# Taking the POOL engine out of the front of a two-block transformer kernel, and spreading its modulation sums

## The chip, the cores and the metric

One core of a Trainium2 chip runs the whole program as one launch. The metric is the device time of a launch in microseconds (us); the kernel before took 2275.55 us (median of 3 runs, 2274.65 to 2276.33).

## The reference

Two blocks follow each other on 256 latent tokens of width 1024. The change lies in the first part of the first block, called the front here: the modulation vectors, the input projection and the two token mixers.

```python
m_l = silu(c) @ w_ada + b_ada                      # 6 x 1024 numbers: shift, scale, gate, twice
u_l = modulate(x, sh1_l, sc1_l) @ w_in             # 256 x 4128; the same for 256 context tokens: u_c
u_c = modulate(ctx, sh1_c, sc1_c) @ w_in
mix_c, mix_l = token_mixer(u_c, u_l, ...)          # HGRN2 (4 heads of 128), GLA (4 heads, in column order)
x = layer_norm(ALPHA * x + g1_l * (mix_l @ w_out), ...)
y_l = peer(modulate(x, sh2_l, sc2_l), ...)         # 16384 experts; then the second block
```

Each mixer is a gated linear recurrence, scanned forwards and backwards over the context and then the latent tokens.

## The kernel before

**Products of three.** Every float32 product is made of three matmuls: weight and activation are each split into a high part, rounded to the matmul's format, and the rest (`hi`, `lo`). The class `Stream` (L251 on) brings all weights in tiles of 128x1024 (512 KB) through one ring of four buffers `raw` and one DMA queue, SP's. `split_to` makes `wh` on ScalarE (L296) and `wl = raw - wh` on VectorE or on POOL (L297), which of the two is the letter "s" or "p" of the tile in `PROJ_MODES`, one pair of letters for each of the 16 groups of 256 columns of `w_in`. A `raw` buffer is free for the next load when its `wl` is made.

**Modulation sums.** The first 2048 columns of `w_ada` are multiplied on TensorE (`ada1_gen`, L521). 24 of the other 32 tiles come through the same ring with mode "r": `ada2_step` (L610) multiplies a tile by the row `crow` on VectorE and sums it along its rows, and its `raw` buffer is free after that. `ADA_PLAN` says after which of the 16 groups how many of these tiles stand; a tile is summed when its group's products are evacuated.

**Projection.** `fm_gen` (L618) makes 256 columns of features, `tm_gen` (L659) 256 columns with tokens on the partitions. The forget gates come first (4 groups of 512 tokens, evacuated at L680 to L684), then the values of the first mixer. The rest (queries, the GLA columns, the output gates) is a chain of generators from which `together` takes one piece, or several, between the steps of the mixers, after the list `FILL`.

**Mixers.** `mixer_states` scans the context, and `mixer` goes through nine levels L = 128, 64, 1, 32, 16, 8, 4, 2, 0. `prep(L)` makes four differences of scanned decays on VectorE (L802 to L805), two exponentials on ScalarE (L806, L807), the product with the keys on VectorE (L811, L812 or L809) and the product of `Qt` with the queries, L820, on POOL. For L = 1 the keys are copied on POOL (L818, L819). `scores` multiplies `Kt` and `Qt` on TensorE (L832) and puts the result into `SB` (L838 on ScalarE, or L840 on VectorE). `decays_g` (L940 to L944) makes the decays of the second mixer in the middle of the first, and L888, L891 write the outputs. After that come the output projection `wout` (from L992), layer norms and the expert stage.

**Column order.** For the GLA part the latent half of the split activations `xh`, `xl` is copied in column order into `hh`, `hl` by 16 casts (L905) on POOL.

**Order of instructions.** The order on each engine is not the program's: a scheduler sets it before the run, and each engine then works in that order, waiting at an instruction until what it reads is there.

Three stages are used below. Stage 1 is 61.65 to 187.30 us (from the first evacuated gate to the first L940), stage 2 to 238.5 us (the first L802 of the second mixer), stage 3 to 299.7 us (the first L992).

Of the kernel before, what the change touches and what calls it, by code (L numbers as in the profile page):

```python
# [8 lines left out]
F32 = mybir.dt.float32  # L9
# [3 lines left out]
AF = mybir.ActivationFunctionType  # L13
OP = mybir.AluOpType
# [9 lines left out]
             "gq": (2560, 256), "gk": (2816, 256), "gv": (3072, 512), "gg": (3584, 512), "gl": (4096, 32)}  # L24
W_IN_ORDER = ("hff", "hfb", "hi", "hq", "gl", "gk", "gq", "gv", "hg", "gg")
N_ADA = 24
ADA_PLAN = (0, 3, 3, 3, 3, 3, 3, 3, 3, 0, 0, 0, 0, 0, 0, 0, 0)

VEC = {}
_n = 0  # L30
# [13 lines left out]
OHB = 4  # L44
MIX_ORDER = 'PPPSPPPSSSSSSSSSMMSSSMSSMMMMMMMMMAASAAAAAPPPAAAPPPPPPPFFFFFPPPPFFFPPPPPPRRVFF'
EARLY = (9, 9, 7)
PROJ_MODES = ['ss', 'ss', 'pp', 'ps', 'sp', 'ss', 'ps', 'ss', 'ss', 'sp', 'pp', 'pp', 'sp', 'pp', 'pp', 'pp']
FILL_N = (8, 9, 17, 37, 53)
MODES = ("sssp", "sssp")
FILL = (3, 4, 1, 4, 3, 4, 2, 6, 5, 3, 3, 0, 0, 1, 3, 1, 3, 2, 2, 1, 2, 1)  # L50
# [125 lines left out]
def build(tc, A, out):  # L176
    nc = tc.nc
    V, S, T, G = nc.vector, nc.scalar, nc.tensor, nc.gpsimd

    with ExitStack() as ctx:  # L180
# [17 lines left out]
        for name in W_IN_ORDER:  # L198
# [3 lines left out]
            for g in range(n // 256):  # L202
                for half in range(2):
                    specs.append((A["win"][gi * 2 + half], PROJ_MODES[gi][half]))
                if gi == 1:
                    specs[1], specs[2] = specs[2], specs[1]
                for _ in range(ADA_PLAN[gi]):
                    specs.append((A["wa2"][na], "r"))
# [140 lines left out]
        def bc(ap, shape):  # L349
            return ap.to_broadcast(shape)  # L350
# [109 lines left out]
        with ExitStack() as fctx:  # L460
# [145 lines left out]
            def ada2_step(c):  # L606
                w = W.get("r")
                j = nada[0]
                nada[0] += 1
                V.scalar_tensor_tensor(w, w, 1.0, c, op0=OP.mult, op1=OP.mult, accum_out=mada[:, 16 + j:17 + j])  # L610

            def ada2_some():
                for _ in range(ADA_PLAN[ngroup[0]]):
                    ada2_step(crow)
                ngroup[0] += 1
# [40 lines left out]
            def colmajor(ap):  # L656
                return ap.rearrange("p (r w) -> p w r", w=64)
# [109 lines left out]
            def mixer(tg, nh, q, ks, a, v, Sc, sc, m0, between={}):  # L767
# [7 lines left out]
                b = []  # L775
# [11 lines left out]
                def prep(L):  # L787
                    Kt = tl("Kt", [4, 256], "Kt", 2)[:, 0:nh]
                    if L:
                        n = 128 // L  # L790
                        Qt = tl("Qt", [4, 256], "Qt", 2)[:, 0:nh]
                        sh = [128, nh, n, L]
                        kf0, _ = halves(ks[0][:, 0], L)
                        _, kb1 = halves(ks[1][:, 0], L)
                        K0, K1 = halves(Kt, L)
                        Q0, Q1 = halves(Qt, L)
                        if L > 1:
                            bf0, bf1 = halves(b[0], L)
                            bb0, bb1 = halves(b[1], L)
                            rf = bc(bf0[:, :, :, L - 1:L], sh)  # L800
                            rb = bc(bb1[:, :, :, 0:1], sh)
                            V.tensor_tensor(K0, rf, bf0, OP.subtract)  # L802
                            V.tensor_tensor(K1, rb, bb1, OP.subtract)
                            V.tensor_tensor(Q1, bf1, rf, OP.subtract)
                            V.tensor_tensor(Q0, bb0, rb, OP.subtract)  # L805
                            S.activation(out=Qt, in_=Qt, func=AF.Exp, scale=sc)  # L806
                            S.activation(out=Kt, in_=Kt, func=AF.Exp, scale=sc)  # L807
                            if same:
                                V.tensor_tensor(Kt, Kt, ks[0][:, 0], OP.mult)  # L809
                            else:  # L810
                                V.tensor_tensor(K0, K0, kf0, OP.mult)  # L811
                                V.tensor_tensor(K1, K1, kb1, OP.mult)  # L812
                        else:
                            _, af1 = halves(a[0][:, 0], L)
                            ab0, _ = halves(a[1][:, 0], L)
                            S.activation(out=Q1, in_=af1, func=AF.Exp, scale=sc)
                            S.activation(out=Q0, in_=ab0, func=AF.Exp, scale=sc)
                            G.tensor_copy(K0, kf0)  # L818
                            G.tensor_copy(K1, kb1)  # L819
                        G.tensor_tensor(Qt, Qt, q, OP.mult)  # L820
                    else:
                        V.tensor_tensor(Kt, ks[0][:, 0], ks[1][:, 0], OP.add)
                        Qt = q
                    return L, Kt, Qt
# [77 lines left out]
            xph, xpl = hh, hl  # L902
            for a, b in ((xph, xh), (xpl, xl)):
                for k in range(8):
                    G.tensor_copy(a[:, k, :].rearrange("p (w r) -> p w r", r=4), colmajor(b[:, k, 0:256].bitcast(F32)))  # L905

            nc.sync.dma_start(wgk, A["wgk"])

# [39 lines left out]
            def gate_ev(gain):  # L948
                def ev(f, ps):
                    if not gate:  # L950
# [8 lines left out]
                              for g in range(2)], gl_gen(), fm_gen(512, ev, 0, 1),  # L959
                            fm_gen(256, lambda f, ps: S.activation(out=gq[:, f, :].rearrange("p (w r) -> p w r", r=4),  # L960
                                                                   in_=colmajor(ps[:, 0:256]), func=AF.Copy, scale=0.125), 0, 2),
# [35 lines left out]
            for k in st1.end(eps1[:, 0:1], [xlat[:, k] for k in range(8)]):  # L997
                n, o, g, b = xlat[:, k], x1[:, k], vc("lng")[:, k:k + 1], bcen[:, k:k + 1]
# [8 lines left out]
            m2, r = tl("m2", [256], "b0"), tl("r2m", [256], "b1")  # L1007
# [16 lines left out]
        with ExitStack() as ectx:  # L1024
# [155 lines left out]
            for i2 in range(128):  # L1180
                hi, lo = W.get("s")
                p = PM()[:, 0:256]
# [37 lines left out]
            p = PS()  # L1220
# [36 lines left out]
            for i2 in range(125):  # L1257
                w = W.get("s")
# [7 lines left out]
            w = [W.get("s") for _ in range(3)]  # L1266
# [524 lines left out]
```

## Time and profile before

| what | before |
|---|---|
| median of 3 runs | 2275.55 us |
| the profiled execution, its own time | 2275.68 us |
| its span, first to last instruction | 2272.9 us |
| PE (matmul) busy | 2174.4 us, 96% |
| VectorE (DVE) busy | 1562.2 us, 69% |
| ScalarE (ACT) busy | 1166.6 us, 51% |
| POOL busy | 490.7 us, 22% |
| mean granted clock of TensorE | 0.981 |

A busy PE is not a PE at its peak: matmuls overlap, and one that waits behind another counts as busy, so work is better read from counts of matmuls. PE is the matmul row of TensorE, PEld its weight loads. The granted clock is a share of full speed (1.00 is 2.4 GHz). "idle" in a group of instructions is the time its engine stood still just before them, with what ended it.

### The profile page before, as it was taken

To read this page: it belongs to the slowest core of one execution; us is meant where nothing else is said; L and a number is where in the kernel's file an instruction comes from. 1 tells how busy PE (TensorE), PEld (TensorE's weight loads), DVE (VectorE), ACT (ScalarE), POOL (GpSimd) and SP (SyncE) were. 2 spreads that over 40 slices of the span, in tenths; PEclk is the share of its full clock that TensorE was granted. 3 is DMA by queue.
4 is the path that set the end of the run, shared out by engine and by line. 5 is a ranking of instruction groups with operands and counts; after the bars stand their busy time and mean duration, and the time that the engine had idled before them with its cause. 6 is when DMAs were issued, how large, how long until landed. Compare 5 with 4: busy or idle time off the path is not lost.

```text
span 2272.9 us, 40224 instructions
## 1 busy us (share of the span) xinstructions
PE 2174.4 (96%) x15660; PEld 2039.1 (90%) x15660; DVE 1562.2 (69%) x2786; ACT 1166.6 (51%) x2016; POOL 490.7 (22%) x464
## 2 busy tenths in 40 slices
PE   6898889899999999999989999999999999899998
PEld 4788779899999998888879999899999999889998
DVE  6897879963778866666665556786557555778554
ACT  4545655344444455555545445675446444676443
POOL 2224422222988810000010002110001000402000
PEclk9999999999999999999999999999999999999999
DMA  6652124555444457666555554344564556234664
GB/s 266 213 186 75 56 84 142 162 177 183 148 142 147 145 182 238 213 194 195 194 183 168 175 175 140 97 149 149 177 179 153 173 170 198 94 120 130 186 180 127
DMA packets 101999, 367.37 MB, mean 162 GB/s; under 512 B 11440, under 2 KB 13360, under 8 KB 100528
## 3 DMA queue, kind: packets, MB, share of 16 engines
q1 hardware_dynamic: 101808, 364.81, 50.6%
q8 instruction: 122, 2.00, 0.4%
q14 instruction: 69, 0.57, 0.1%
HBM read 363.72 MB, written 1.05 MB: 160 GB/s over the span
## 4 chain that ended last, share of the span: by engine, by line
PE 78%; DVE 12%; issue 3%; ACT 3%; POOL 2%; DMA 2%; SPq 0%; DVEq 0%; POOLq 0%; ACTq 0%
PE main L336 18%; PE main L335 18%; PE main L334 18%; PE aux L1254 5%; PE aux L1256 5%; PE aux L1255 5%; DVE wl L297 3%; PE aux L1144 3%; DVE raw L610 1%; POOL wl L297 1%; ACT wh L296 1%; PE aux L832 1%; DVE X L1076 1%; DVE X L1074 1%; DMA raw<-wa 1%
## 5 line engine op out<-in xcount | busy, mean ns | idle before, releaser
L296 ACT ACTIVATE wh<-raw 128x1024 fp32r<-128x1024 f32 (+1 forms) x630 | 659.4, 1047 | 702.0 <-PE main L335 348.0
L297 DVE TENSOR_TENSOR wl<-raw,wh 128x1024 fp32r<-128x1024 f32 (+1 forms) x589 | 724.9, 1232 | 382.0 <-ACT wh L296 381.5
L336 PE MATMUL main<-hh,wl 128*128 128x256 f32 (+1 forms) x2808 | 806.7, 288 | 20.3 <-DVE wl L297 19.9
L334 PE MATMUL main<-hh,wh 128*128 128x256 f32 (+1 forms) x2808 | 810.5, 289 | 12.2 <-DVE hh L444 6.1
L335 PE MATMUL main<-hl,wh 128*128 128x256 f32 (+1 forms) x2808 | 805.4, 287 | 1.5 <-DVE hl L448 0.7
L336 PEld LDWEIGHTS main<-hh,wl 128*128 128x128 f32 x2808 | 534.7, 190 | 26.1 <-DVE wl L297 23.7
L334 PEld LDWEIGHTS main<-hh,wh 128*128 128x128 f32 x2808 | 533.8, 190 | 16.8 <-DVE hh L444 7.0
L335 PEld LDWEIGHTS main<-hl,wh 128*128 128x128 f32 x2808 | 532.9, 190 | 3.8 <-DVE hl L448 2.0
L396 POOL TENSOR_TENSOR acc<-acc,sqk 128x272 f32<-128x272 f32 (+1 forms) x29 | 37.2, 1284 | 1207.6 <-ACT sqk L389 1207.5
L1138 POOL TENSOR_SCALAR oh<-cst,slotT 128x128 f32<-128x128 f32 x256 | 209.1, 832 | 38.4 <-PE aux L1144 32.6
L334 PE MATMUL main<-ah,wh 128*128 128x272 f32 (+1 forms) x704 | 201.7, 286 | 0.0
L335 PE MATMUL main<-al,wh 128*128 128x272 f32 (+1 forms) x704 | 201.3, 286 | 0.0
L336 PE MATMUL main<-ah,wl 128*128 128x272 f32 (+1 forms) x704 | 200.6, 285 | 0.0
L1254 PE MATMUL aux<-wh,xsh 128*128 128x512 f32 x512 | 199.3, 390 | 0.0
L1255 PE MATMUL aux<-wl,xsh 128*128 128x512 f32 x512 | 199.3, 389 | 0.0
L1256 PE MATMUL aux<-wh,xsl 128*128 128x512 f32 x512 | 199.2, 389 | 0.0
L297 POOL TENSOR_TENSOR wl<-raw,wh 128x1024 fp32r<-128x1024 f32 x41 | 112.9, 2755 | 302.1 <-ACT wh L296 301.4
L339 ACT ACTIVATE xsh<-X 128x256 fp32r<-128x256 f32 x128 | 53.7, 420 | 165.8 <-PE aux L1255 163.9
L336 PEld LDWEIGHTS main<-ah,wl 128*128 128x128 f32 x704 | 132.4, 188 | 0.0
L334 PEld LDWEIGHTS main<-ah,wh 128*128 128x128 f32 x704 | 132.3, 188 | 0.0
L335 PEld LDWEIGHTS main<-al,wh 128*128 128x128 f32 x704 | 132.2, 188 | 0.0
L1255 PEld LDWEIGHTS aux<-wl,xsh 128*128 128x128 f32 x512 | 96.1, 188 | 20.3 <-DVE wl L297 0.3
(507 smaller groups left out, 3246.0 us busy)
## 6 DMA issues: line engine op xcount, KB each, us to landing
raw<-uT SPq DMA_DIRECT2D x128, 512.0 KB, 3.6
raw<-pv SPq DMA_DIRECT2D x128, 512.0 KB, 4.2
raw<-ffn_gate SPq DMA_DIRECT2D x88, 512.0 KB, 3.6
raw<-ffn_up SPq DMA_DIRECT2D x88, 512.0 KB, 3.7
raw<-win SPq DMA_DIRECT2D x72, 512.0 KB, 3.7
raw<-ffn_down SPq DMA_DIRECT2D x64, 512.0 KB, 3.6
raw<-wa SPq DMA_DIRECT2D x32, 512.0 KB, 4.5
raw<-wout SPq DMA_DIRECT2D x24, 512.0 KB, 3.6
```

The costliest lines, as they stand in the source:

```text
L296: S.activation(out=hi[:, :n], in_=t[:, :n], func=AF.Copy)
L297: (G if mode == "p" else V).tensor_tensor(lo[:, :n], t[:, :n], hi[:, :n].bitcast(F32), OP.subtract)
L334: T.matmul(o, lh, rh, start=start, stop=False)
L335: T.matmul(o, lh, rl, start=False, stop=False)
L336: T.matmul(o, ll, rh, start=False, stop=stop)
L339: S.activation(out=hi, in_=src, func=AF.Copy)
L396: (G if self.k < (5 if self.pe == 7 else 2) else V).tensor_tensor(self.acc2, self.acc2, q, OP.add)
L1138: G.tensor_scalar(oh1[:, j], iota, slotT[0][:, t0 + j:t0 + j + 1], None, op0=OP.is_equal)
L1144: T.matmul(pg[:, 128 * j:128 * j + 128], oh1[:, j], oh2[:, j], start=True, stop=True)
L1254: T.matmul(y, x[0][:, c], w[0][:, f], start=(i2 == 0), stop=False)
L1255: T.matmul(y, x[0][:, c], w[1][:, f], start=False, stop=False)
L1256: T.matmul(y, x[1][:, c], w[0][:, f], start=False, stop=(i2 == 127))
```

## The change

`PROJ_MODES` becomes "ss" for all 16 groups: the 17 `wl` of the projection that POOL made go to VectorE. L820 goes to VectorE, the two key copies of L = 1 and the 16 casts of L905 to ScalarE. `ADA_PLAN` had three sums after each of groups 1 to 8, and has one after groups 1 to 4 and two after groups 5 to 14, 24 as before. Up to the end of stage 3 POOL keeps only one multiplication of the input normalisation (L580).

```diff
-ADA_PLAN = (0, 3, 3, 3, 3, 3, 3, 3, 3, 0, 0, 0, 0, 0, 0, 0, 0)
+ADA_PLAN = (0, 1, 1, 1, 1, 2, 2, 2, 2, 2, 2, 2, 2, 2, 2, 0, 0)
...
-PROJ_MODES = ['ss', 'ss', 'pp', 'ps', 'sp', 'ss', 'ps', 'ss', 'ss', 'sp', 'pp', 'pp', 'sp', 'pp', 'pp', 'pp']
+PROJ_MODES = ['ss'] * 16
...
-                            G.tensor_copy(K0, kf0)
-                            G.tensor_copy(K1, kb1)
-                        G.tensor_tensor(Qt, Qt, q, OP.mult)
+                            S.activation(out=K0, in_=kf0, func=AF.Copy)
+                            S.activation(out=K1, in_=kb1, func=AF.Copy)
+                        V.tensor_tensor(Qt, Qt, q, OP.mult)
...
             for a, b in ((xph, xh), (xpl, xl)):
                 for k in range(8):
-                    G.tensor_copy(a[:, k, :].rearrange("p (w r) -> p w r", r=4), colmajor(b[:, k, 0:256].bitcast(F32)))
+                    S.activation(out=a[:, k, :].rearrange("p (w r) -> p w r", r=4), in_=colmajor(b[:, k, 0:256].bitcast(F32)), func=AF.Copy)
```

The order on the engines moves with it. The first piece is VectorE at the start of stage 1, where the first gates are evacuated (L682, L684 scale `gat` and `kx`); "-" is the order before, "+" the new one:

```order
-L610 SCALAR_TENSOR_TENSOR raw,mada<-raw,crow 128x1024 x3
+L297 TENSOR_TENSOR wl<-raw,wh 128x1024 x2
+L610 SCALAR_TENSOR_TENSOR raw,mada<-raw,crow 128x1024
 L682 TENSOR_SCALAR gat_113<-gat_113,lbt 128x2x256
 L684 TENSOR_SCALAR kx_115<-kx_115,lbt 128x2x256
 L682 TENSOR_SCALAR gat_113<-gat_113,lbt 128x2x256
```

Three sums stood ahead of the second group's gates; now two splits and one sum do. By the first L940, VectorE's order has 19 splits and 14 sums where it had 11 and 24, and six L820.

The second place is VectorE at level L = 16 of the first mixer, late in stage 1. Before:

```order
L802 TENSOR_TENSOR Kt<-bl_1164 128x32x16
L803 TENSOR_TENSOR Kt<-bl_1169 128x32x16
L804 TENSOR_TENSOR Qt<-bl_1164 128x32x16
L805 TENSOR_TENSOR Qt<-bl_1169 128x32x16
L811 TENSOR_TENSOR Kt<-Kt,kx_115 128x32x16
L812 TENSOR_TENSOR Kt<-Kt,kx_116 128x32x16
L840 COPY_PREDICATED SB<-msk,aux 128x4x128 x2
```

Now:

```order
L802 TENSOR_TENSOR Kt<-bl_1131 128x32x16
L803 TENSOR_TENSOR Kt<-bl_1136 128x32x16
L804 TENSOR_TENSOR Qt<-bl_1131 128x32x16
L805 TENSOR_TENSOR Qt<-bl_1136 128x32x16
L297 TENSOR_TENSOR wl<-raw,wh 128x1024
L811 TENSOR_TENSOR Kt<-Kt,kx_115 128x32x16
L812 TENSOR_TENSOR Kt<-Kt,kx_116 128x32x16
L820 TENSOR_TENSOR Qt<-Qt,q_hg 128x1024
L840 COPY_PREDICATED SB<-msk,aux 128x4x128 x2
```

A split and the product with the queries now stand in VectorE's own row of work, the product just ahead of the previous level's L840.

The third place is VectorE in stage 2, ahead of L888, which writes the first mixer's output. Before:

```order
L822 TENSOR_TENSOR Kt<-kx_115,kx_116 128x1024
L854 TENSOR_TENSOR bl_1169<-bl_1169,q_hg 128x1024
L840 COPY_PREDICATED SB<-msk,aux 128x4x128 x4
L888 TENSOR_TENSOR x_99<-r_1862,aux 128x256 x2
L731 SCALAR_TENSOR_TENSOR R<-ones_679,la 128x256 x2
```

Now:

```order
L840 COPY_PREDICATED SB<-msk,aux 128x4x128 x2
L297 TENSOR_TENSOR wl<-raw,wh 128x1024
L610 SCALAR_TENSOR_TENSOR raw,mada<-raw,crow 128x1024
L297 TENSOR_TENSOR wl<-raw,wh 128x1024
L610 SCALAR_TENSOR_TENSOR raw,mada<-raw,crow 128x1024 x3
L888 TENSOR_TENSOR x_99<-r_1840,aux 128x256 x2
```

Two splits and four sums, each of which waits for its load, now stand between the last L840 and L888. In all, stage 2 has 6 splits, 8 sums and 2 L820 on VectorE (before: 1, 0, 0), and stage 3 has 7, 2 and 8 (before: 3, 0, 0).

## Rows read from the trace of the kernel before

**Rows 1.** Windows: length, busy (count) of PE, PEld, DVE, ACT, POOL; clock, DMA, GB/s

```profile
61.65:187.30 125.65, 108.49 (x673) 97.87 (x672) 118.83 (x146) 63.56 (x86) 41.72 (x17) 0.94 0.58 189
187.30:238.50 51.20, 50.51 (x361) 45.70 (x361) 36.08 (x53) 27.92 (x45) 17.36 (x8) 0.95 0.17 52
238.50:299.70 61.20, 51.84 (x405) 44.63 (x404) 47.35 (x98) 33.39 (x72) 24.54 (x14) 0.92 0.20 61
500.00:525.00 25.00, 25.00 (x213) 25.00 (x213) 7.36 (x6) 11.62 (x17) 6.87 (x3) 1.00 0.58 181
840.00:900.00 60.00, 60.00 (x267) 49.67 (x266) 42.21 (x56) 30.31 (x45) 0.00 (x0) 1.00 0.72 237
```

**Rows 2.** VectorE groups by form, stage 1: xcount | busy us, mean ns | idle before

```profile
L610 DVE SCALAR_TENSOR_TENSOR raw<-raw,crow 128x1024 f32<-128x1024 f32 x24 | 35.1, 1491 | 5.1 <-DMA raw<-wa 5.0
...
L803 DVE TENSOR_TENSOR Kt<-bl 128x512 f32<-128x512 f32 x5 | 9.9, 1985 | 0.0
...
L812 DVE TENSOR_TENSOR Kt<-Kt,kx 128x512 f32<-128x512 f32 x5 | 5.6, 1117 | 0.0
L804 DVE TENSOR_TENSOR Qt<-bl 128x512 f32<-128x512 f32 x5 | 5.6, 1113 | 0.0
L802 DVE TENSOR_TENSOR Kt<-bl 128x512 f32<-128x512 f32 x5 | 5.5, 1099 | 0.0
```

**Rows 3.** VectorE in order of time, 159 to 165 us: start us, length us

```profile
159.11 1.22 DVE L610 SCALAR_TENSOR_TENSOR raw<-raw,crow 128x1024 f32<-128x1024 f32 x1
...
160.70 1.22 DVE L297 TENSOR_TENSOR wl<-raw,wh 128x1024 fp32r<-128x1024 f32 x1
161.84 0.68 DVE L802 TENSOR_TENSOR Kt<-bl 128x512 f32<-128x512 f32 x1
162.44 2.85 DVE L803 TENSOR_TENSOR Kt<-bl 128x512 f32<-128x512 f32 x1
```

**Rows 4.** POOL in order of time, 162 us

```profile
162.36 2.38 POOL L297 TENSOR_TENSOR wl<-raw,wh 128x1024 fp32r<-128x1024 f32 x1 [4.26 <-ACT wh L296]
```

**Rows 5.** POOL groups by form, all three stages

```profile
L297 POOL TENSOR_TENSOR wl<-raw,wh 128x1024 fp32r<-128x1024 f32 x17 | 47.3, 2785 | 67.5 <-ACT wh L296 67.2
L820 POOL TENSOR_TENSOR Qt<-Qt,q_hg 128x1024 f32<-128x1024 f32 x8 | 20.8, 2612 | 51.4 <-ACT Qt L806 51.4
L820 POOL TENSOR_TENSOR Qt<-Qt,gq 128x512 f32<-128x512 f32 x8 | 12.3, 1539 | 14.5 <-ACT Qt L806 11.4 <-PE main L336 2.5 <-ACT Qt L817 0.6
```

**Rows 6.** Waits in stage 1, ScalarE for weight loads: us, times, longest

```profile
ACT wh L296 <- DMA raw<-win: 31.2, 9, 7.1
```

**Rows 7.** TensorE groups by form, stage 1, the 512-column kinds

```profile
L334 PE MATMUL main<-xh,wh 128*128 128x512 f32 x56 | 22.1, 394 | 0.0
...
L334 PE MATMUL aux<-xh,wh 128*128 128x512 f32 x8 | 3.3, 416 | 0.0
```

**Rows 8.** VectorE groups by form, stage 2

```profile
L854 DVE TENSOR_TENSOR bl<-bl,q_hg 128x1024 f32<-128x1024 f32 x2 | 4.0, 2004 | 0.0
...
L822 DVE TENSOR_TENSOR Kt<-kx,kx 128x1024 f32<-128x1024 f32 x1 | 2.8, 2753 | 0.0
```

**Rows 9.** Waits in stage 2, VectorE

```profile
DVE x L888 <- ACT r L344: 6.7, 1, 6.7
```

**Rows 10.** VectorE groups by form, stage 3

```profile
L802 DVE TENSOR_TENSOR Kt<-bl 128x256 f32<-128x256 f32 x7 | 8.1, 1153 | 3.9 <-PE aux L832 3.9
...
L981 DVE TENSOR_TENSOR x<-x,gate 128x256 f32<-128x256 f32 x8 | 5.1, 659 | 0.0
...
L805 DVE TENSOR_TENSOR Qt<-bl 128x256 f32<-128x256 f32 x7 | 2.9, 418 | 0.0
```

**Rows 11.** Waits in stage 3, TensorE for POOL

```profile
PE aux L832 <- POOL Qt L820: 7.7, 3, 3.5
```

**Rows 12.** ScalarE in order of time, 33 to 43 us

```profile
42.31 0.60 ACT L525 ACTIVATE row<-aux 128x512 f32<-128x512 f32 x1 [8.78 <-PE aux L521]
```

**Rows 13.** ScalarE groups by form, all three stages

```profile
L339 ACT ACTIVATE hh<-x 128x256 fp32r<-128x256 f32 x8 | 3.1, 417 | 7.1 <-DVE x L981 6.9
```


## The prediction

> **What bounds the kernel now.** I first read the windows: how busy each engine is in a stretch, and at what clock. In the two dense stretches, from 480 us on for most of the run, TensorE never rests: 213 matmuls in 25 us, 117 ns each, and 267 of 512 columns in 60 us, 225 ns each, at a granted clock of 1.00 [rows 1]. The change touches nothing there, so I read the three stages of the front. In stage 1, VectorE is occupied for 118.8 of 125.65 us, 94.6%, while TensorE's 673 matmuls are 99.5 us of work: 192 write 512 columns (56 and 8 on each of three lines, of which one stands in [rows 7]; 192 x 225 ns = 43.2 us), 481 are smaller (481 x 117 ns = 56.3 us). So VectorE sets the pace, and TensorE has 26 us to spare. In stage 2 VectorE is busy 36.1 of 51.2 us and TensorE has 361 x 117 ns = 42.2 us; in stage 3 it is 47.4 of 61.2 us and 405 x 117 ns = 47.4 us [rows 1]. Nobody rules these two alone; the clock of 0.92 to 0.95 says that TensorE was let down at times.
>
> The second view, VectorE's groups, shows what fills its 118.8 us. L803 takes 1985 ns on average and L610 1491 ns [rows 2], though the order of time has an L802 of the same shape at 0.68 us and an L610 at 1.22 us [rows 3]. The L803 beside that L802 took 2.85 us: it began at 162.44, just after POOL began a split of 2.38 us at 162.36 [rows 3, 4]. VectorE stood through POOL's instruction and then did its own work.
>
> **The change, part by part.**
>
> What VectorE gets back. For each group the count times the mean above its undisturbed length: in stage 1, L610 24 x (1.49 - 1.22) = 6.5 us, L803 5 x (1.99 - 0.68) = 6.5, L812 2.2, L804 2.1, L802 2.1, together 19.4 us [rows 2, 3]; in stage 2, against 1.22 us for 1024 columns, L854 2 x 0.79 and L822 1.53, together 3.1 [rows 3, 8]; in stage 3, against 0.42 us as L805 has it, L802 7 x 0.74 and L981 8 x 0.24, together 7.1 [rows 10]. That is 29.6 us, and smaller groups are left out. The Trainium skill, SBUF — State Buffer, "Who interferes with whom", says that a VectorE instruction with two SBUF inputs and a GpSimd instruction that reads SBUF exclude each other, and that whichever comes second waits for the whole of the first. By that rule the return could be all of POOL's 83.6 us in the three stages; the rows have a third of it, and I take the rows.
>
> What VectorE is given. One instruction of 1024 columns costs 1.14 us of its time: an L297 starts at 160.70 and the next instruction at 161.84 [rows 3]. For the moved splits, 17, and the eight L820 of 1024 columns [rows 5] that is the price; the eight of 512 columns cost 0.60 us, as L802 does (161.84 to 162.44 [rows 3]). No lower price is likely, and the highest is 1.22 us, the full length. POOL took 2.79, 2.61 and 1.54 us for the same [rows 5]. With the new order: stage 1 gets 8 splits and 6 L820 and loses 10 sums, (8 + 6 - 10) x 1.14 = +4.6 us; stage 2 gets 5 splits, 8 sums and 2 L820, 15 x 1.14 = +17.1; stage 3 gets 4 splits, 2 sums and 8 short L820, 6 x 1.14 + 8 x 0.60 = +11.6.
>
> VectorE's occupied time then goes from 118.8 to 118.8 - 19.4 + 4.6 = 104.0 us in stage 1, from 36.1 to 50.1 in stage 2, from 47.4 to 51.9 in stage 3.
>
> Stage 1. If VectorE keeps its share of 94.6%, the stage takes 104.0 / 0.946 = 110 us, **16 us less**. TensorE's 99.5 us fit into that at 90%, and no better than 99.5 is possible: the gain lies between 0 and 26 us. Fewer tiles pass through the ring of `raw` in the stage as well, 33 in place of 44 (11 + 9 splits and 24 sums before, 19 and 14 after), so ScalarE's 31.2 us of waits for weights [rows 6] should shrink; I count nothing more for that, since it is the same gain seen from another engine.
>
> Stage 2. The 17.1 us must fit into VectorE's 15.1 us of idle time, of which 6.7 are the wait of L888 for ScalarE [rows 9], ahead of which the two splits and four sums now stand. Between -3 (the stalls alone count) and +14 (50.1 - 36.1, nothing fits): I take **+2**, near the fitting end, since the new order puts the work where VectorE waits. What is late if it does not fit is L888, and behind it the second mixer's first scans.
>
> Stage 3. TensorE waits 7.7 us for POOL's L820 [rows 11]; VectorE makes the 512 columns in 0.60 instead of 1.54 us, but in a queue with 4.5 us more of work, and three of the eight L981 are now done after the levels rather than between them. Between -8 and +5: I take **-2**.
>
> ScalarE gets 16 casts and four copies. A cast of 128x256 is nearest to L339, 0.42 us [rows 13], so 16 are 6.7 us; the copies are under 3 us by the same row, scaled. Eight casts stand before L525 at 42.31 us, which waits 8.8 us for TensorE [rows 12]; 8 x 0.42 = 3.4 us fit there. The other eight stand among the first gates, where ScalarE is half idle (63.6 of 125.65 us [rows 1]). I cost them at nothing; without that cover each batch is 3.4 us. The loads keep their order on SP but for the sums' tiles, which come later; POOL's own queue loses everything in the stages.
>
> The sum is -16 + 2 - 2 = -16 us on the profiled execution of 2275.68 us, which is 0.13 us above the median: about **2259.5 us**. A measurement of this kernel can tell 0.2% from no change, some 4.5 us.
>
> **The rivals.**
>
> A larger gain: VectorE leaves the path of stage 1 altogether and TensorE's count is all that remains (-25), the clock stays up, stage 2 costs nothing (-1) and stage 3 gives the whole wait for POOL (-7): -33, 2242.5 us. For it: the three stages run at 0.92 to 0.95 of the clock [rows 1], and a TensorE that rests less would be let down less. Against: the mixers' steps depend on each other through three engines, and TensorE at 99% has no room for that.
>
> No change that can be told: the returned time turns into waits for weights. ScalarE's 31.2 us [rows 6] are set by the four buffers of the ring and the time a load takes; if that goes on, stage 1 gains 4 us only, and with +2 - 2 the sum is -4, 2271.5 us. Against: these waits end later because sums and POOL's splits hold the buffers, and both get out of the way.
>
> Slower: stages 2 and 3 become VectorE's. Its idle time there may be latency that added work cannot use, because the order is fixed and a sum that waits for its load holds up L888 or an L802 behind it. Then stage 2 costs the full +14 and stage 3 the full 51.9 - 47.4 = +4.5, and if stage 1 gives 12 the sum is +6.5, 2282 us. It decides where less than about 4 us of the 17.1 fit into waits. For it: 50.1 of 51.2 us is a fuller queue than stage 1's is now. Against: the six instructions ahead of L888 meet a wait of 6.7 us [rows 9].
>
> The change does not give back what I think: the long VectorE instructions have another cause, and stay. Then stage 1 pays all of its 4.6 us, and stages 2 and 3 their 17.1 and 11.6 less half of their idle time of 15.1 and 13.9 [rows 1]: 4.6 + 9.6 + 4.7 = +19, 2294.5 us. The Trainium skill, Perfetto Trace Analysis, "Optimizing Scalar/DVE Operations", would have work taken off a saturated VectorE, even to GPSIMD; by that alone this change goes the wrong way, though the page adds that the two share a port and moving between them might not help. Against: the 2.85 us beside 2.38 us on POOL [rows 3, 4].
>
> **How the numbers follow.** The forecast, with stage 1 between -9 and -24, gets 0.55; the larger gain 0.14; no change 0.13; VectorE-bound mixers 0.15; the stalls that stay 0.03. Faster by over 0.2% is the first two, 0.69; within 0.2% is 0.13; slower 0.18. The range from 2247 to 2278 us takes in the forecast's, the no-change case and the shallow part of the larger gain; outside lie the slower cases and the deepest gains, about 0.2.
>
> **What would show it.** Right: L803 and L802 of 512 columns at 0.68 to 0.70 us throughout, L610 near 1.22, the first L940 on VectorE some 16 us earlier, near 171 us, the first L802 of the second mixer near 225, and the first L992 near 284; ScalarE's waits for weights well under 31 us; no POOL instruction between 60 us and the layer norm after `wout`. Wrong: long L803 without POOL; L888 or L802 waiting behind sums that wait for their loads; stage 2 over 60 us. From 300 us on every distance between instructions should be as before; a difference there would be of another cause than mine.

## The result, and the profile after

The changed kernel takes **2249.95 us** (median of 4 runs, 2249.63 to 2250.39) where the kernel before, beside it, took 2275.32 us (4 runs, 2274.65 to 2276.33). The ratio is 0.9888, with a 95% interval of 0.9876 to 0.9900: 25.4 us or 1.1% faster, inside the range of the prediction, 3 us above its lower end, and 9.5 us below its number. The profiled execution took 2249.63 us, its span is 2247.57; before, the span was 2272.95.

The windows of the changed kernel come first, cut at the same instructions as before (first L682, first L940, first L802 of the second mixer, first L992) and at one more, ScalarE's first L1172, behind which the search stage begins. Columns are those of [rows 1].

```profile
0.00:57.52 57.52, 41.06 (x192) 26.51 (x193) 38.44 (x85) 31.58 (x52) 3.59 (x5) 0.91 0.69 272
57.52:168.71 111.19, 105.50 (x681) 95.12 (x681) 95.93 (x138) 69.67 (x97) 0.00 (x0) 0.98 0.50 161
168.71:218.89 50.18, 48.81 (x353) 44.61 (x352) 48.27 (x76) 27.18 (x45) 0.00 (x0) 0.97 0.47 147
218.89:277.58 58.69, 52.33 (x405) 44.95 (x404) 50.97 (x116) 33.58 (x73) 0.00 (x0) 0.88 0.27 82
277.58:320.24 42.66, 34.19 (x225) 30.81 (x224) 32.69 (x70) 25.82 (x45) 14.06 (x16) 0.96 0.33 102
```

The kernel before has, ahead of stage 1 and behind stage 3, these two windows, which stand in no group above:

```profile
0.00:61.65 61.65, 42.30 (x192) 27.00 (x193) 43.90 (x85) 27.22 (x44) 17.49 (x21) 0.89 0.65 254
...
299.71:344.04 44.33, 36.79 (x225) 32.83 (x224) 32.71 (x70) 26.03 (x45) 14.29 (x16) 0.88 0.31 98
```

Side by side, with the forecast:

| stretch | before | after | difference | forecast |
|---|---|---|---|---|
| ahead of stage 1 | 61.65 | 57.52 | -4.1 | 0 |
| stage 1 | 125.65 | 111.19 | -14.5 | -16 |
| stage 2 | 51.2 | 50.2 | -1.0 | +2 |
| stage 3 | 61.2 | 58.7 | -2.5 | -2 |
| L992 to L1172 | 44.3 | 42.7 | -1.7 | 0 |
| the rest | 1928.9 | 1927.3 | -1.6 | 0 |

VectorE's groups in stage 1, to be read against [rows 2]: every length is now the undisturbed one, and the splits and queries that POOL did in 2785 and 2612 ns [rows 5] take 1218 to 1220.

```profile
L297 DVE TENSOR_TENSOR wl<-raw,wh 128x1024 fp32r<-128x1024 f32 x20 | 24.2, 1218 | 1.4 <-ACT wh L296 1.4
L610 DVE SCALAR_TENSOR_TENSOR raw<-raw,crow 128x1024 f32<-128x1024 f32 x14 | 17.0, 1219 | 7.0 <-DMA raw<-wa 7.0
L820 DVE TENSOR_TENSOR Qt<-Qt,q_hg 128x1024 f32<-128x1024 f32 x6 | 7.3, 1220 | 0.0
...
L803 DVE TENSOR_TENSOR Kt<-bl 128x512 f32<-128x512 f32 x5 | 3.4, 685 | 0.0
L802 DVE TENSOR_TENSOR Kt<-bl 128x512 f32<-128x512 f32 x5 | 3.4, 679 | 0.0
```

Of the waits in stage 1, ScalarE's for weights, 31.2 us before [rows 6], is nearly gone:

```profile
ACT wh L296 <- DMA raw<-win: 4.6, 3, 2.6
```

For what follows I add up, over all VectorE instructions of a stretch, how far each is longer than the median of its line and shape in the changed kernel, and call the sum the **stalls**. Before, they were 7.8 us ahead of stage 1, then 27.1, 4.3 and 8.2 in the stages; after, 2.2 us are left ahead of stage 1, all of them in one L580 (see the first norm below), and nothing beyond 0.2 us in any stage. Two groups of stage 1 in the kernel before that hold 4 us of this and stand in no group above (beside undisturbed lengths of 543 and 482 ns in the changed kernel):

```profile
L682 DVE TENSOR_SCALAR gat<-gat,lbt 128x512 f32<-128x512 f32 x8 | 6.1, 766 | 0.1
L684 DVE TENSOR_SCALAR kx<-kx,lbt 128x512 f32<-128x512 f32 x8 | 6.0, 745 | 0.0
```

### The profile page after: what moved, and what is told of

Read it like the earlier page. It is cut to its first block, busy times and chain, and to the rows that moved or that the text cites. A ratio compares the mean times of both kernels' runs of the same rounds, so it can differ in the third digit from the quotient of the medians.

```text
span 2247.6 us, 40177 instructions
## 1 busy us (share of the span) xinstructions
PE 2167.5 (96%) x15660; PEld 2034.8 (91%) x15660; DVE 1546.6 (69%) x2819; ACT 1174.9 (52%) x2036; POOL 391.6 (17%) x411
## 3 DMA queue, kind: packets, MB, share of 16 engines
q1 hardware_dynamic: 101808, 364.81, 51.2%
## 4 chain that ended last, share of the span: by engine, by line
PE 79%; DVE 14%; ACT 3%; issue 3%; DMA 1%; POOL 1%; SPq 0%; DVEq 0%; POOLq 0%; ACTq 0%
PE main L336 19%; PE main L335 18%; PE main L334 18%; PE aux L1255 5%; PE aux L1254 5%; PE aux L1256 5%; DVE wl L297 3%; PE aux L1144 3%; DMA raw<-wa 1%; DVE X L1076 1%; DVE X L1074 1%; DVE SB L840 1%; DVE Qt L820 1%; DVE X L1073 0%; DVE X L1075 0%
## 5 line engine op out<-in xcount | busy, mean ns | idle before, releaser
L297 DVE TENSOR_TENSOR wl<-raw,wh 128x1024 fp32r<-128x1024 f32 (+1 forms) x606 | 741.0, 1224 | 382.4 <-ACT wh L296 381.9
L1254 PEld LDWEIGHTS aux<-wh,xsh 128*128 128x128 f32 x512 | 96.0, 188 | 20.2 <-ACT wh L296 0.3
```

The costliest lines, as they stand in the source:

```text
L297: (G if mode == "p" else V).tensor_tensor(lo[:, :n], t[:, :n], hi[:, :n].bitcast(F32), OP.subtract)
L1254: T.matmul(y, x[0][:, c], w[0][:, f], start=(i2 == 0), stop=False)
```

## The experiments

The theory: VectorE stands while POOL reads SBUF, and the time is won because POOL is gone. The rivals: the sums' new places and the loads behind them make the gain, or the new order of the instructions does, whatever POOL does. Each kernel was compared with the kernel before in the same session. The first table has the measured times, the second the length of each stretch in the profiles (us).

| kernel | median, us | ratio to before | 95% interval |
|---|---|---|---|
| changed | 2249.95 | 0.9888 | 0.9876 to 0.9900 |
| sums alone | 2273.61 | 0.9997 | 0.9988 to 1.0006 |
| splits alone | 2269.05 | 0.9977 | 0.9967 to 0.9987 |
| casts alone | 2273.61 | 0.9993 | 0.9984 to 1.0002 |
| queries alone | 2274.88 | 1.0002 | 0.9993 to 1.0011 |
| changed, sums undone | 2252.84 | 0.9897 | 0.9882 to 0.9912 |
| changed, splits undone | 2264.15 | 0.9952 | 0.9939 to 0.9966 |
| changed, queries undone | 2264.22 | 0.9950 | 0.9936 to 0.9964 |
| changed, casts undone | 2254.34 | 0.9905 | 0.9888 to 0.9922 |
| changed, idle POOL reads | 2266.39 | 0.9963 | 0.9949 to 0.9976 |
| changed, later splits too | 2246.15 | 0.9869 | 0.9853 to 0.9886 |
| changed, first norm too | 2245.68 | 0.9871 | 0.9854 to 0.9887 |
| changed, both | 2247.56 | 0.9876 | 0.9860 to 0.9893 |

| kernel | ahead | stage 1 | stage 2 | stage 3 | to L1172 | rest |
|---|---|---|---|---|---|---|
| before | 61.7 | 125.6 | 51.2 | 61.2 | 44.3 | 1928.9 |
| sums alone | 62.3 | 120.1 | 56.6 | 60.1 | 44.3 | 1927.9 |
| splits alone | 62.2 | 122.0 | 52.5 | 60.3 | 42.6 | 1927.8 |
| casts alone | 57.5 | 127.2 | 51.8 | 60.6 | 45.5 | 1929.1 |
| queries alone | 62.3 | 122.7 | 54.1 | 61.5 | 44.3 | 1928.7 |
| changed | 57.5 | 111.2 | 50.2 | 58.7 | 42.7 | 1927.3 |
| sums undone | 58.0 | 118.0 | 48.0 | 55.4 | 44.3 | 1925.5 |
| splits undone | 58.3 | 114.7 | 57.7 | 56.4 | 44.3 | 1927.9 |
| queries undone | 57.3 | 117.9 | 56.7 | 56.2 | 44.3 | 1925.6 |
| casts undone | 62.1 | 108.9 | 51.3 | 58.2 | 44.3 | 1928.6 |
| idle POOL reads | 57.7 | 114.1 | 56.2 | 66.7 | 42.6 | 1927.6 |
| later splits too | 57.7 | 109.1 | 50.3 | 58.0 | 44.3 | 1925.2 |
| first norm too | 54.8 | 108.7 | 51.9 | 58.7 | 42.6 | 1927.3 |
| both | 55.4 | 109.6 | 52.0 | 58.3 | 44.3 | 1925.2 |

The last two columns show what to leave out of account: from L992 to L1172 a kernel takes 42.6 or some 44.3 us (one 45.5), at a granted clock of 0.96 or 0.85 to 0.92, and the rest swings between 1925.5 and 1929.1 among the kernels that change nothing there. The 3.2 us that the change gained there are of that kind; some 22 us belong to the front up to L992. Single stages swing as well: the changed kernel and the four whose VectorE and TensorE have the same work in stages 1 and 2 (casts undone and the last three) take 108.7 to 111.2 us for stage 1 and 50.2 to 52.0 for stage 2, so a difference of 2 us in one stage of one profile says little.

### Each part alone

**The sums alone.**

```diff
-ADA_PLAN = (0, 3, 3, 3, 3, 3, 3, 3, 3, 0, 0, 0, 0, 0, 0, 0, 0)
+ADA_PLAN = (0, 1, 1, 1, 1, 2, 2, 2, 2, 2, 2, 2, 2, 2, 2, 0, 0)
```

> The kernel before with the new plan of the sums alone (ADA_PLAN over 14 groups); POOL keeps its splits, queries and casts. The theory of stalls (VectorE stands through POOL's instructions, and the sums are plain VectorE time): ten sums leave stage 1, 10 x 1.14 = 11 us of VectorE's time, so stage 1 shrinks by 8 to 12 us; eight go to stage 2 and two to stage 3, where they cost 0 to 4 us; together -5 to -10 us, and L803 of 512 columns stays far above 0.68 us. The rival of the loads (the ring of raw buffers was the bound, and spreading the sums is the whole change): -18 us or more, ScalarE's waits for win fall from 31.2 us to about 5.

Measured: no difference. Stage 1 lost 5.6 us, where 8 to 12 were expected, and stage 2 grew by 5.4, where stages 2 and 3 were to cost 0 to 4: my theory had both sizes wrong. The rival of the loads is out, and in a telling way, for its sign came and its gain did not. ScalarE's waits for weights in stage 1 fell from 31.2 us to

```profile
ACT wh L296 <- DMA raw<-win: 2.5, 1, 2.5
```

and the kernel was no faster for it.

**The splits alone.**

```diff
-PROJ_MODES = ['ss', 'ss', 'pp', 'ps', 'sp', 'ss', 'ps', 'ss', 'ss', 'sp', 'pp', 'pp', 'sp', 'pp', 'pp', 'pp']
+PROJ_MODES = ['ss'] * 16
```

> The kernel before with all 17 splits of the projections on VectorE (PROJ_MODES) and nothing else. The theory of stalls: in stage 1 VectorE takes 8 x 1.14 = 9 us and gets back the part of its stalls that stood beside splits, some 17 us, so -6 to -10 us there, about 0 in stages 2 and 3; together -5 to -11 us. The rival of the loads: 0 within 3 us, since the sums still fill the ring. A third reading, that VectorE's queue is all that counts and POOL's work was free: +9 us in stage 1, +5 or more overall.

Measured: -5.7 us, the weak end of what was expected. In stage 1 the stalls went from 27.1 to 12.4 us, while nine splits more took 10.9; the stage became 3.7 us shorter, where 6 to 10 were expected.

**The casts alone.**

```diff
-                    G.tensor_copy(a[:, k, :].rearrange("p (w r) -> p w r", r=4), colmajor(b[:, k, 0:256].bitcast(F32)))
+                    S.activation(out=a[:, k, :].rearrange("p (w r) -> p w r", r=4), in_=colmajor(b[:, k, 0:256].bitcast(F32)), func=AF.Copy)
```

> The kernel before with the 16 casts of L905 on ScalarE and nothing else; the order on TensorE, VectorE and SP is unchanged, and no weight passes another way. The theory of stalls: L562 falls from 0.72 to 0.40 us, L563 from 1.12 to 0.68, and all that follows stage 1's first L682 begins some 4 us earlier, which stays to the end: -3 to -5 us. A rival by which a new order of the instructions, and not POOL's standing in the way, made the 4.1 us ahead of stage 1: 0 within 1 us, or slower by the 7 us that ScalarE is given. The prediction on record costed this part at nothing.

Measured: -1.2 us, which can't be told from none; the 3 to 5 us expected did not come. But the first L682 came 4.1 us earlier, at 57.51. The groups of VectorE between 29 and 62 us, in the kernel before:

```profile
L563 DVE TENSOR_TENSOR xl<-xm,xh 128x512 fp32r<-128x512 f32 x8 | 6.9, 876 | 0.1
...
L562 DVE TENSOR_SCALAR xm<-xn,mada 128x256 f32<-128x256 f32 x8 | 5.3, 658 | 0.0
```

and between 29 and 58 us with the casts alone:

```profile
L563 DVE TENSOR_TENSOR xl<-xm,xh 128x512 fp32r<-128x512 f32 x8 | 5.4, 684 | 0.3 <-ACT xh L561 0.2
...
L562 DVE TENSOR_SCALAR xm<-xn,mada 128x256 f32<-128x256 f32 x8 | 3.2, 405 | 0.0
```

The order on TensorE, VectorE and SP is the same row for row in both, so the 4.1 us come from taking the casts off POOL. Of them 1.5 us went again in stage 1, and 1.2 us in the stretch from L992 to L1172, at a clock of 0.85; both are no larger than the swings named above.

**The queries alone.**

```diff
-                        G.tensor_tensor(Qt, Qt, q, OP.mult)
+                        V.tensor_tensor(Qt, Qt, q, OP.mult)
```

> The kernel before with the sixteen L820 (the mixers' queries scaled) on VectorE and nothing else. The theory of stalls: in stage 1 six instructions of 1.14 us, 7 us, are paid and some 9 us of stalls come back, -2; in stage 3 TensorE's 7.7 us of waits for POOL's L820 shrink by some 4 us; together -3 to -7 us. The rival of the loads: about 0 in stage 1 and only stage 3's wait, -2 to -4 us. POOL's work was free: +7 in stage 1 and +3 overall or more.

Measured: no gain, where 3 to 7 us were expected. Stage 1 lost 3.0 us, stage 2 grew by 2.9, and stage 3, where most of the gain was expected, did not shrink. The four parts come to -8 us alone (1.2 + 5.7 + 1.2 - 0.1), the whole change to -25.4. The table says where the missing 17 us lie. Summed over the four parts, stage 1 changed by -10.8 us (the whole change: -14.5), stage 2 by +10.2 (-1.0) and stage 3 by -2.3 (-2.5). So some 15 of them are in stages 1 and 2: what the sums or the queries alone took from stage 1 came back in stage 2. Why was the question for the next kernels.

### One part undone, and POOL's presence by itself

**Sums undone** (the changed kernel with the old `ADA_PLAN`):

> The changed kernel with the old plan of the sums (three in each of eight groups). If the parts add up as they measured alone (sums -1, splits -5, casts -1, queries 0, together -7), the whole change's other 18 us come from the parts being together, and taking one away should cost far more than it gave alone. Theory of complements: the sums leave stage 1, where VectorE is nearly full, for stage 2, where its time is free only once POOL's splits no longer stand in its way; ten sums of 1.14 us come back into stage 1, which grows by 4 to 10 us, stage 2 becomes 0 to 3 us shorter: 2253 to 2259 us. Rival, parts that simply add: 2251 us, and the 18 us must then come from pairs of the others.

Measured 2252.84 us, 2.9 above the changed kernel; the intervals overlap. Both theories gave about this, so it does not tell them apart, but its profile prices the sums' new places: with the old plan stage 1 is 6.8 us longer, stage 2 is 2.2 shorter and stage 3 is 3.3 shorter.

**Splits undone** (the changed kernel with the old `PROJ_MODES`):

> The changed kernel with the 17 splits back on POOL; queries, casts and sums as in the change. Theory of complements: stage 1 gets back some 15 us of VectorE's stalls less 10 us of work, +4 to +6; in stage 2 the sums meet POOL's splits as they do with the sums moved alone, +4 to +6; stage 3 +1 to +3; together 2259 to 2266 us. Rival, parts that add: +5, 2255 us.

**Queries undone** (the changed kernel with `G.tensor_tensor(Qt, Qt, q, OP.mult)`):

> The changed kernel with the sixteen L820 back on POOL. Theory of complements: 7 us of stalls in stage 1 less 5 us of work, where VectorE now has 15 us of idle time: +1 to +4; stages 2 and 3 +3 to +6, with TensorE waiting for L820 again; together 2254 to 2260 us. Rival, parts that add: 2250 us, no change.

Measured: 2264.15 and 2264.22 us, 14.2 and 14.3 above the changed kernel, where the parts alone had given 5.7 and 0. The first is as expected, the second above the 2254 to 2260 expected. The parts don't add: each is worth most where the others have been done. The profiled execution of each was the fastest of its five, 2261.22 and 2260.84 us, so some 3 us of each loss stand in no profile. Of what the profiles show, 11.7 and 10.5 us, stage 2 has 7.5 and 6.5 and stage 1 has 3.6 and 6.8; stage 3, which was expected to grow, is 2.3 and 2.5 us shorter than in the changed kernel. The window of stage 2 in the two kernels, first with the splits undone:

```profile
173.01:230.66 57.65, 51.76 (x366) 46.67 (x366) 47.35 (x74) 26.86 (x46) 12.20 (x4) 0.95 0.36 119
```

then with the queries undone:

```profile
175.28:231.94 56.66, 51.94 (x359) 47.09 (x359) 49.48 (x75) 27.13 (x45) 7.98 (x2) 0.92 0.39 121
```

The kernels of the table form a square for stage 2. With the sums in it and any POOL instructions (sums alone, splits undone, queries undone, idle reads) it takes 56.2 to 57.7 us; with the sums and no POOL, 50.2 to 52.0 in five kernels; without the sums, 51.2 to 54.1 with POOL and 48.0 with none. Taking POOL out is worth 3 to 6 us there without the sums and 4 to 7.5 with them: eight sums leave VectorE little room to stand (48.27 of 50.18 us busy in the changed kernel). What TensorE waits for in the stage agrees: L832 waits 3.4 to 3.6 us for L820 with the sums alone, the splits undone or the queries undone, 2.2 with the idle reads, and 0.2 in the changed kernel. How this adds up to the 14 us was not taken apart further.

**Idle POOL reads.** The changed kernel, and on the same 17 tiles that POOL used to split, a POOL subtraction whose result nobody reads:

```diff
+IDLE_MODES = ['ss', 'ss', 'pp', 'ps', 'sp', 'ss', 'ps', 'ss', 'ss', 'sp', 'pp', 'pp', 'sp', 'pp', 'pp', 'pp']
...
+                            c in idle and G.tensor_tensor(fp.tile([128, 1024], F32, tag="idle", name="idle", bufs=1), hi.bitcast(F32), hi.bitcast(F32), OP.subtract)
```

> The changed kernel with 17 POOL subtractions added whose results nobody reads, on the same 17 tiles that POOL split before (hi minus hi, into a tile of their own); the order on TensorE, VectorE, ScalarE and SP is the same row for row, and no engine waits for POOL's results. Theory of stalls: VectorE's 512- and 1024-column instructions become long again beside them, some 15 us of stalls in stage 1 and 6 in stages 2 and 3; stage 1 has 15 us of idle VectorE time to take part of it: +8 to +18 us, 2258 to 2268. Rival, the new order and not POOL's absence made the gain: 2250 us within 2.

Measured: 2266.39 us, 16.4 above the changed kernel, with the order on the other four engines the same row for row, and in the three stages no engine waits for POOL. This is the direct price of POOL's presence, and the rival, by which the new order made the gain, is out. In order of time, POOL and then VectorE:

```profile
233.89 1.90 POOL L297 TENSOR_TENSOR idle<-wh 128x1024 f32<-128x1024 f32 x1 [17.73 <-ACT wh L296]
...
234.30 2.03 DVE L809 TENSOR_TENSOR Kt<-Kt,gk 128x512 f32<-128x512 f32 x1 [0.38 <-ACT Kt L807]
```

L809 of this shape takes 0.69 us earlier in the same stage (at 230.83); here it began inside POOL's read, which ended at 235.79, and ended 0.54 us behind it. Its windows:

```profile
57.73:171.87 114.14, 104.91 (x681) 95.15 (x680) 108.61 (x137) 69.38 (x97) 21.45 (x9) 0.98 0.49 157
171.87:228.07 56.20, 50.43 (x338) 45.25 (x339) 53.80 (x76) 25.85 (x41) 10.38 (x4) 0.89 0.42 131
228.07:294.77 66.70, 56.52 (x421) 49.09 (x418) 55.79 (x117) 34.98 (x76) 8.13 (x4) 0.84 0.23 72
```

40.0 us of POOL's reads made VectorE's busy time 23.0 us longer for the same work (12.7, 5.5 and 4.8 in the stages, against the changed kernel's windows). Stage 1, where VectorE had 15 us to spare, took all but 3 of its share; stages 2 and 3 lost 6 and 8 us, at a clock that fell to 0.89 and 0.84. The Trainium skill (SBUF — State Buffer, "Who interferes with whom") has the rule that of a VectorE instruction with two SBUF inputs and a GpSimd (POOL) instruction that reads SBUF the second waits for the whole of the first. By it, as an estimate, up to 40 us of stalls were possible; the pair at 234 us agrees with it, and the sum is lower. Part of the reason is in the kept trace: not all of VectorE's instructions stand. Up to 299.7 us of the kernel before, L840, which reads a result of TensorE (`aux`), began 25 times inside an instruction of POOL, at least 0.2 us before its end, and kept its length each time (711 to 758 ns for 512 columns, 438 to 458 for 256); L802 of the second mixer and the first began 6 times so and took 1.7 to 2.5 us each time.

**One place where two parts are worth more than their sum: the start of the second mixer.** It lies at the start of stage 3, so it is not where the missing 17 us are, but it shows in small how two causes hold up one wait. In order of time, VectorE's first L802, the first L820 (POOL or VectorE) and TensorE's first L832, which needs both. The kernel before:

```profile
238.51 2.53 DVE L802 TENSOR_TENSOR Kt<-bl 128x256 f32<-128x256 f32 x1
...
243.04 3.76 POOL L820 TENSOR_TENSOR Qt<-Qt,gq 128x512 f32<-128x512 f32 x2 [2.28 <-ACT Qt L806]
...
245.18 2.08 PE L832 MATMUL aux<-Qt,Kt 64*128 64x128 f32 x16 [3.52 <-POOL Qt L820]
```

The splits alone:

```profile
236.63 0.40 DVE L802 TENSOR_TENSOR Kt<-bl 128x256 f32<-128x256 f32 x1
...
238.84 2.87 POOL L820 TENSOR_TENSOR Qt<-Qt,gq 128x512 f32<-128x512 f32 x1 [27.91 <-DVE Kt L803]
...
241.76 2.01 PE L832 MATMUL aux<-Qt,Kt 64*128 64x128 f32 x16 [2.46 <-POOL Qt L820]
```

The queries alone:

```profile
239.12 2.53 DVE L802 TENSOR_TENSOR Kt<-bl 128x256 f32<-128x256 f32 x1
...
243.86 0.68 DVE L820 TENSOR_TENSOR Qt<-Qt,gq 128x512 f32<-128x512 f32 x1
...
244.68 2.08 PE L832 MATMUL aux<-Qt,Kt 64*128 64x128 f32 x16 [2.05 <-DVE Qt L820]
```

Splits, queries and casts together (sums undone):

```profile
223.94 0.40 DVE L802 TENSOR_TENSOR Kt<-bl 128x256 f32<-128x256 f32 x1
...
226.53 0.68 DVE L820 TENSOR_TENSOR Qt<-Qt,gq 128x512 f32<-128x512 f32 x1
...
227.36 1.16 PE L832 MATMUL aux<-Qt,Kt 64*128 64x128 f32 x16
```

From the first L802 to the first L832 it takes 6.67, 5.13, 5.56 and 3.42 us. In the first three TensorE waits 3.52, 2.46 and 2.05 us, having done the projections that stand ahead of L832 in its order; then its clock is down (0.50 to 0.52 over the next 3 us), and the same 16 matmuls take 2.0 to 2.1 us. In the fourth it waits for nothing that the row shows, and they take 1.16. Two windows of 3 us, the kernel before:

```profile
241.05:244.05 3.00, 0.61 (x6) 0.40 (x4) 3.00 (x9) 2.63 (x7) 1.01 (x1) 0.95 0.58 175
244.05:247.05 3.00, 1.87 (x16) 1.78 (x16) 3.00 (x3) 1.23 (x5) 2.75 (x2) 0.50 0.00 0
```

and the changed kernel at the same place:

```profile
222.42:225.42 3.00, 2.74 (x35) 2.45 (x32) 3.00 (x7) 3.00 (x9) 0.00 (x0) 1.00 0.03 5
```

One part alone shortens the wait, and the clock behind it is still down at its lower level, 1.2 GHz; both together, with the casts, end the wait and keep the clock. But these two parts are not all that counts here. With the splits or the queries undone in the changed kernel, so that the sums are spread as well and the casts gone, the same row reads

```profile
234.42 1.16 PE L832 MATMUL aux<-Qt,Kt 64*128 64x128 f32 x16 [0.58 <-DVE Qt L820]
```

and

```profile
236.46 1.16 PE L832 MATMUL aux<-Qt,Kt 64*128 64x128 f32 x16 [1.57 <-POOL Qt L820]
```

at a clock of 1.00 behind it: a short wait is left, and the clock stays up. So this place can account for a part of what splits and queries give together without the sums (stage 3 changes by -0.9 and +0.3 us alone, and by -5.8 with splits, queries and casts), and for at most 0.6 and 1.6 of the 14 us by which the two undone kernels are slower. That other places work alike was not shown.

### The casts, and what POOL still does

**Casts undone** (the changed kernel with L905 on POOL again):

> The changed kernel with the 16 casts of L905 back on POOL. Alone the casts brought the first L682 forward by 4.1 us, and three of these were lost by 300 us. Theory: they are lost only where VectorE and POOL hold each other up later, so in the changed kernel, without POOL in the stages, the 4 us stay to the end: 2253 to 2255 us. Rival, the gain ahead of stage 1 is swallowed by the chain behind it whatever POOL does: 2250 to 2251.5 us.

Measured 2254.34 us, +4.4, as the theory had it: the slowest run of the changed kernel, 2250.39, is below the fastest of this one, 2253.07, though the intervals of the ratios overlap. The first L682 is at 62.09, 4.6 us later, with L562 and L563 as long as in the kernel before, and most of it stays.

**The later splits too.**

```diff
-MODES = ("sssp", "sssp")
+MODES = ("ssss", "ssss")
```

> The changed kernel with the splits of the following stage (every fourth tile of wq and uT, 14 of them on POOL between 278 and 490 us) on VectorE as well. VectorE is occupied 24 to 25 of every 25 us from 345 to 445 us there, mostly by its search instructions of one input, and its instructions stand only some 8 us longer than undisturbed. Theory, by the account of returned stalls against 1.14 us per split: it gets back some 6 us and pays 9 to 12: slower, +2 to +7 us, 2252 to 2257. Rival, any work is better taken off POOL: -3 to -8 us, 2242 to 2247.

Measured 2246.15 us (2244.55 to 2247.30): not slower, so my theory fell. From the first L1172 to the first L1141, where the search ends, eleven of the kernels here take 222.5 or 222.6 us, the changed kernel's profile 220.5, and this kernel 219.2. VectorE was counted as busy there, but its groups between 390 and 482 us in the changed kernel

```profile
L297 DVE TENSOR_TENSOR wl<-raw,wh 128x1024 fp32r<-128x1024 f32 x23 | 30.0, 1310 | 17.2 <-ACT wh L296 17.2
L1113 DVE TENSOR_TENSOR X<-X 128x2048 f32<-128x2048 f32 x4 | 11.0, 2753 | 0.0
```

and with the later splits on VectorE

```profile
L297 DVE TENSOR_TENSOR wl<-raw,wh 128x1024 fp32r<-128x1024 f32 x32 | 38.7, 1222 | 11.0 <-ACT wh L296 11.0
L1113 DVE TENSOR_TENSOR X<-X 128x2048 f32<-128x2048 f32 x4 | 9.2, 2291 | 0.0
```

show that L1113 had stood 0.46 us each time, and that VectorE waited for ScalarE's casts of weights, time in which the nine splits more found room. I had counted the price of the added work in full and the idle time not at all.

**The first norm too.**

```diff
-                        E = G if a and e and st is rstd else V
+                        E = V
```

> The changed kernel with the one normalisation that POOL still does ahead of stage 1 (L580, 3.4 us at 25 us) on VectorE, which has 19 us of idle time there. Theory: VectorE pays 1.2 us and gets back at most 0.2 us of stalls, but the modulation behind it no longer waits for POOL: -0 to -2 us. Rival: no difference within 1 us, because the projections wait for the loads of the weights.

Measured 2245.68 us (2245.06 to 2248.27), 4.3 below the changed kernel, where 0 to 2 were expected. In the changed kernel POOL's and VectorE's last L580 ran side by side, and both took 3.4 us:

```profile
23.66 3.39 POOL L580 TENSOR_TENSOR xctx<-xctx,rstd 128x1024 f32<-128x1024 f32 x1 [23.22 <-ACT rstd L344]
...
24.76 3.38 DVE L580 TENSOR_TENSOR xctx<-xctx,rstd 128x1024 f32<-128x1024 f32 x1
```

With both on VectorE:

```profile
24.65 1.22 DVE L580 TENSOR_TENSOR xctx<-xctx,rstd 128x1024 f32<-128x1024 f32 x1
```

All behind it comes 2.8 us earlier, up to the first L682 at 54.77. I had expected the gain from what waits for POOL and at most 0.2 us of stalls; it was a stall of 2.16 us.

**Both.**

> The changed kernel with both edits that measured below it: the normalisation L580 and the remaining 18 splits of wq and uT on VectorE. In the profiles the first brought all behind 25 us forward by 2.8 us, the second the stretch from 390 to 481 us by some 3.5 us, of which 2.4 us hold against the start of the search stage. Theory, two separate places: the gains add, -5 to -7 us against the changed kernel, 2243 to 2245 us. Rival, the first gain is lost ahead of the search stage or there (VectorE is full from 345 to 445 us and waits for nothing that comes earlier): 2246 us, as either alone.

Measured 2247.56 us (2245.14 to 2248.23), where 2243 to 2245 were expected: no sum of the two shows. The 2.1 us that it gains up to the first L682, and a search of 219.2 us (1.3 below the changed kernel's, 3.3 below the others'), are in its profile, but from L992 to L1172 it took 44.3 us at a clock of 0.88, where the changed kernel had 42.7 at 0.96. All three kernels have a median 2.4 to 4.3 us below the changed kernel's, near the 0.2% that a comparison can tell, and their intervals overlap with its own. The first norm alone is the best candidate for a better version; that it is one is likely, and not settled.

## Why the prediction was right, and where its steps were not

**What bounds.** That POOL's instructions make VectorE long, and that this costs the kernel time, was right: the idle POOL reads show it with nothing else changed. The sign rested on this. That VectorE set the pace of stage 1 is shown less directly: the stage became 14.5 us shorter when VectorE's occupied time in it fell by 22.9, but only 5.6 when the sums alone took some 11 off it. The marks that it named came as told: L803 and L802 at 0.68 us, L610 at 1.22, no POOL instruction in the stages, the first L940 at 168.7 (near 171 was named), the second mixer's first L802 at 218.9 (225), the first L992 at 277.6 (284).

**Stage 1, -16, measured -14.5: two errors that nearly cancel.** The returned time, "together 19.4 us" with "smaller groups" left out, was too low: the stalls were 27.1 us, and none are left. Some of the groups left out were about as large as some that were counted: L682 and L684 had 1.8 and 2.1 us, L744, a copy of 4 columns, 2.2. So VectorE's occupied time fell to 95.9 us, not 104.0. At the share assumed, that would have been a stage of 101 us. But the step "If VectorE keeps its share of 94.6%" failed: it keeps 86%, for it no longer sets the pace. TensorE is now busy 105.5 of 111.2 us, 95%, as VectorE was. Of the 22.9 us that VectorE was relieved of, 8.4 became its idle time. The floor that the prediction named, TensorE's 99.5 us, was nearer than the share allowed for.

**Stage 2, +2, measured -1.0.** The sums cost 2.2 us there (50.2 against 48.0 with them undone), but splits and queries off POOL gave 3.2 (51.2 to 48.0). The 17.1 us did fit, since stalls of 4.1 us, not 3.1, came back and nearly all of the 15.1 us of idle time could be used: 1.9 are left, and L888 no longer waits there. The rival of VectorE-bound mixers was close: VectorE is busy 48.3 of 50.2 us, and with POOL instructions beside that the stage takes 56 to 58 us (the rival had 65).

**Stage 3, -2, measured -2.5.** TensorE waits 5.3 us for VectorE's L840 where it waited 7.7 for POOL [rows 11]:

```profile
PE aux L832 <- DVE SB L840: 5.3, 3, 2.6
```

The stage's clock is 0.88, lower than before. With the sums undone the stage is 55.4 us at 0.94. The size was right by chance, for the clock was no part of the sum.

**The casts, "I cost them at nothing": wrong, 4.1 us.** The step looked for the cover on ScalarE, which takes the work over, and not on VectorE beside POOL, where the work was. The rows for it were there: L562 at 658 and L563 at 876 ns, against 405 and 684. ScalarE's price was off too (680 ns each, not 417) and did not matter.

**From 300 us on, "every distance between instructions should be as before":** 3.2 us less, in a stretch and a remainder that swing by as much among kernels which differ nowhere near.

**The no-change rival,** waits for weights, is out: 31.2 us became 4.6, and when spreading the sums alone took them to 2.5 it gave nothing. Of the larger gain's -33 its own terms gave -18: -14.5 of -25 in stage 1, -1.0 of -1 in stage 2, -2.5 of -7 in stage 3. What it rested on, the clock, came in part: in stages 1 and 2 it rose from 0.94 and 0.95 to 0.98 and 0.97, in stage 3 it fell.

**The 9.5 us between the number and the time:** 2 are the three stages (-18 for -16), 4.1 the casts, and 3.2 the stretches behind L992, which swing by as much without it.

**What the sum could not show:** the four parts don't add. Alone they give 8 us. It came out near because its terms were stages, each with all parts in it.

## What to carry to other kernels

Where VectorE is full and POOL has SBUF work beside it, read the same form of VectorE instruction with and without POOL at its side before calling POOL's work free; here 1024 columns cost VectorE 1.14 us to do, and up to 2.2 us to stand beside. Judge such a change as a whole and by undoing its parts, not by adding parts alone: here they gave 8 us alone and 25 together, and at one place TensorE's clock stayed down behind a wait that one part alone had only shortened. And look for the cover of a moved instruction at the place that it leaves, not only where it goes.

## What was not expected of the hardware

POOL is held up by VectorE too: L820 of 512 columns took 2.87 us on POOL at 238.84 in the kernel with the splits alone, and 1.27 to 1.28 us at 244 to 246 us in the same kernel, and POOL's L580 above took 3.39 us where its shortest L820 of 1024 columns in the kernel before took 2.36. VectorE's L562, L682 and L684, whose inputs are one tile and columns of scalars, stood beside POOL too: L562 658 ns against 405 beside the casts, L684 once 2.62 us against 0.48 beside a split. And the price of a short wait of TensorE is not the wait alone: behind 2.05 us at the start of the second mixer, in the kernel with the queries alone, the next 16 matmuls took 2.08 us where they take 1.16 at full clock.
